# Twelve fewer products on TensorE: two blocks of the last recurrent head by Strassen's method, five steps of the recurrence shortened, token sums two blocks at once

## The chip, the cores and the metric

The kernel runs on one core of one Trainium2 chip. A core has five engines, each with its own instruction queue: TensorE (PE in the profile; its weight loads are shown apart as PEld), VectorE (DVE), ScalarE (ACT), GpSimd (POOL) and SyncE (SP), which issues nearly all DMAs. The engines run beside each other and wait for each other through semaphores; each queue is worked off strictly in the order in which it was written. The metric is device time in microseconds, from the first to the last instruction and the little that lies around it. Lower is better.

## The reference: what is computed

One layer of a hybrid encoder on 1024 tokens of width 1024, in float32. One wide projection of the tokens feeds two branches. Branch A is attention with 8 heads of 64 and a forget bias. Branch B is a gated linear recurrence with 4 heads of 128 channels:

```
f = lb + (1 - lb) * sigmoid(f_b)          # forget gate, per head and channel
q = silu(q_b);  k = 1 - f;  v = i_b
S_t = diag(f_t) S_(t-1) + k_t v_t^T;  o_t = S_t^T q_t
o = o * rsqrt(mean(o^2) + eps) * norm_g * sigmoid(g_b)
merged = sigmoid(gate_a) * (y_a @ w_pa) + sigmoid(gate_b) * (y_b @ w_pb)
x1 = layer_norm(ALPHA * x + merged @ w_o)
out = layer_norm(ALPHA * x1 + (silu(x1 @ w_g) * (x1 @ w_u)) @ w_ff_out)
```

The float32 products are made of three products of reduced-precision halves: each operand is split into a high part (`hi`, a cast on ACT) and a remainder (`lo`, a subtraction on DVE), and `mm3` adds hi·hi, hi·lo and lo·hi in PSUM.

## The kernel before

Tokens lie along the free dimension, 512 per PSUM bank, and channels on the 128 partitions. Most matrix products use one level of Strassen's method: seven products of half size in place of eight, with sums of operands made beforehand by DVE. Per block of 128 output channels and all 1024 tokens a direct projection takes 2 token halves x 8 channel chunks x 3 = 48 matmuls of 128x512; two blocks taken together by Strassen's method take 7 products x 4 chunks x 3 = 84 in place of 96.

The program in order of its source:

- values for both branches (`v_mul`), forget gates;
- `qk_all` (L799): four Strassen steps (`qk_strassen`, L733), one for each pair of attention heads. A step pairs a query block with a key block of `w_qk`. It loads the two weight blocks (tags `hl` or `kb`, as `QORDER` says), makes seven stationary operands `Tqk...` (each a cast on ACT and a subtraction on DVE), adds the partial results and writes split queries and keys to DRAM (`qk_d`), from where each attention head loads them again;
- attention by head: scores (`s`), minimum, exponential and row sums (`p`), transposes (`pt`), and the weighted values (`pv`);
- the recurrence by head: `hgrn_project` (L906) projects forget gate (block 1), query (block 0) and output gate (block 2) directly into banks `bps1`, `bps0`, `bps2`; `hgrn` (L934) forms cumulative log gates `b` by scans (eight of 128 tokens), then pair terms on seven levels (`level`, L975, each with four products `lp` that are put into `at` under a mask; the last level, neighbouring tokens, is `neighbours`, L1000), state terms (`up`, `box`) and outputs (`op`), which are normed (`ob`) and transposed (`ot`). Heads 0 to 3 follow each other, with `hgrn_project` of the next head between;
- parts of the merge gates (`gate_part`, `ge`), the rest of them by Strassen (`gs`);
- branch projections (`pps`), gating, and `merged` (L1256), which splits the token sums into operands for the output projection, one 128-channel block at a time; the output projection (`oa`, `ob`), layer norm and transposes (`x1t`), the feed-forward part (`fa` to `fe`, then `p`).

The source order is not the order on the engines. Every call is recorded by `Plan`, with the tiles it reads and writes. `schedule` places all calls by a table of costs (cost per operation, a delay of 400 ns before each TensorE call that depends on another engine, DMAs one after another); `improve` (L355) does this 36 times with ranks from the latest allowed start and random slack, and keeps the order that ends first by these costs. That order is then written out, engine by engine. So any change of the calls, or of the random seed, moves instructions nearly everywhere. Buffers are reused by tag: a new tile of a tag waits until an old one has been read for the last time.

Since each call is issued by one helper, nearly all instructions carry the same line, L387 (L388 after the change); tiles tell them apart. A float32 matmul that is not a transpose is shown as two records.

Of the kernel before, what the change touches and what calls it, by code (L numbers as in the profile page):

```python
# [9 lines left out]
BF16 = mybir.dt.bfloat16  # L10
U16 = mybir.dt.uint16
AF = mybir.ActivationFunctionType
# [51 lines left out]
class Plan:  # L64
# [326 lines left out]
def trunk(ctx: ExitStack, tc, a: dict, out: bass.AP):  # L391
# [340 lines left out]

    def qk_strassen(p, wtags, btags, last=False):  # L733
# [16 lines left out]

        def put(b, hf, o):
            hi, lo = (half("gt" if n else "tt", f"qk{p}_{b}{hf}{n}", F32R) for n in range(2))
            if b == 0:
                act.activation(hi, o, AF.Copy, scale=-0.125)
                dve.scalar_tensor_tensor(lo, o, -0.125, f(hi), op0=ALU.mult, op1=ALU.subtract)
            else:
                split(hi, lo, o)
            for n, t in enumerate((hi, lo)):
                sync.dma_start(qk_d[p, 2 * b + n, :, hs(hf)], f(t))

# [38 lines left out]
    def qk_all():  # L799
        for p, w, b in QORDER:  # L800
            qk_strassen(p, (w, w), b, p == QORDER[-1][0])

# [79 lines left out]

    once = keep([P, P + 1], "once", F32R)
    raw = half("gt", "once_r")
    sync.dma_start(raw[:, :P + 1], a["once"])
    act.copy(once, raw[:, :P + 1])
    reset, ones = f(once)[:, :P], once[:, 1:]
    lmask = const("lmask", [P, 2, MASKS], U16, "mask")
# [45 lines left out]
    def hgrn(h, qfg, box):  # L934
# [40 lines left out]
        def level(li):  # L975
# [17 lines left out]

            if li:
                m = lmask[:, :, 4 * nw - 7:8 * nw - 7, None].to_broadcast([P, 2, 4 * nw, L])
            else:
                m = lmask[:, :, :1, None].to_broadcast([P, 2, 4, L])
            dve.copy_predicated(across(at, L, 1), m, halves(lp, L))

        def neighbours():  # L1000

            low = take("hl", [2, NB], f"nb{h}", F32R)
            hi, lo = low[:, 0, :], low[:, 1, :]
            pr, e = (half("ph", f"nb{n}{h}") for n in "pe")
            b2 = b.rearrange("p (n a) -> p n a", a=2)
# [52 lines left out]
        for hf in range(2):  # L1058
# [197 lines left out]
    def merged(c, k, hf):  # L1256
        if not k and hf:
            return
        r11, r21 = (mraw[0][:, c, hs(i)] for i in range(2))
        r12, r22 = (mraw[1][:, c, hs(i)] for i in range(2))  # L1260
        op = (M11, M12, M22)[k + hf]
        split(op[0][:, c], op[1][:, c], (r11, r12, r22)[k + hf])
        if k and hf:
            s1 = half("tt", f"ms1r{c}")
            dve.tensor_add(s1, r21, r22)
            split(MS1[0][:, c], MS1[1][:, c], s1)
            dve.tensor_sub(r22, s1, r11)
            dve.tensor_sub(r12, r12, r22)
            dve.tensor_sub(r21, r11, r21)
# [100 lines left out]
    for i in (1,):  # L1370
# [6 lines left out]
        for fb in range(KC):  # L1377
# [5 lines left out]
            for hf in range(2):  # L1383
                sg = gated(i, fb, hf)
                o = bank(CYC[nbank % 5], f"pps{i}_{fb}_{hf}")
                nbank += 1
                project(o, w, hf, 4, lambda c: (yh[c], yl[c]))
                dve.tensor_mul(sg, o, sg)
                dve.tensor_add(mf[:, hs(hf)], mf[:, hs(hf)], sg)
                merged(fb % 4, fb // 4, hf)  # L1390
            if fb == 3:
# [88 lines left out]
    def from_raw(name, r):  # L1480
        op = operand("x", name)
        for c in range(4):
            split(op[0][:, c], op[1][:, c], r(c))
        return op
# [416 lines left out]
def _constants():  # L1901
# [3 lines left out]
    causal = np.tile(np.concatenate([causal, causal.T], axis=1), (1, NT // 2))  # L1905
    once = np.ones((P, P + 1), np.float32)
    once[:, 0] = 0
    lmask = np.zeros((P, 2, MASKS), np.uint16)
    for L in LEVELS:
# [86 lines left out]
```

## Time and profile before

| | |
|---|---|
| Median of 3 runs | 1412.66 us (1412.26 to 1413.19) |
| Profiled execution: its time, its span | 1412.1 us, 1410.3 us |
| Mean granted TensorE clock | 0.999 |
| PE, DVE, ACT, POOL busy share | 99%, 82%, 50%, 6% |
| First projection steps for attention (85 to 160 us) | PE 75.00, DVE 52.00, ACT 35.99 us busy |
| Attention (160 to 316 us) | PE 155.48, DVE 132.75, ACT 133.21 us busy |
| Recurrence (316 to 498 us) | PE 182.00, DVE 165.41, ACT 132.52 us busy |
| DMA | 245.23 MB, 174 GB/s on average |

The stages are cut where the trace shows the first score products, the last attention split and the end of the last recurrent head. Busy times of one engine are to be set against the length of the stage. The chain of work that ended last has 79% of the span on PE by the page's summary and DVE with 1%; the remaining pieces are short.

### The profile page before, as it was taken

Reading aid. Unit: us, or ns where it says so; the run is one execution under the profiler, and the core shown is the slowest. Engines: PE = TensorE matmul, PEld = TensorE weight load, DVE = VectorE, ACT = ScalarE, POOL = GpSimd, SP = SyncE. Lnnn points to the kernel's source line nnn. Section 1 sums busy time; section 2 is a strip of 40 time slices with the busy share of each in tenths; the row PEclk is TensorE's granted clock in tenths of the full one; section 3 lists DMA queues with packets and bytes.
Section 4 is the critical chain, followed back from the end, with each engine's and each line's share of the span. In section 5 each row is a group of like instructions: output and inputs, shape, how many; then the busy total and the mean of one; then the engine's idle time right before and its main releaser. Section 6 shows DMA issues by size and latency. Waiting matters only on the chain.

```text
span 1410.3 us, 19118 instructions
## 1 busy us (share of the span) xinstructions
PE 1399.7 (99%) x6650; PEld 1162.8 (82%) x6650; DVE 1161.6 (82%) x2025; ACT 710.5 (50%) x1275; POOL 87.3 (6%) x108
## 2 busy tenths in 40 slices
PE   9999999999999999999999999999999999999997
PEld 7788888888888888888887888888888888888886
DVE  7995878899998979778998879877687976699597
ACT  5534689887687632365439842233223334434330
POOL 0000133420000000000001000000000000000001
PEclk9999999999999999999999999999999999999999
DMA  7458999811113686456644637533334336878632
GB/s 274 156 167 271 301 291 259 243 61 45 46 53 113 215 254 196 134 165 220 231 131 140 208 103 227 181 117 100 98 106 141 112 112 209 315 249 284 216 122 90
DMA packets 99503, 245.23 MB, mean 174 GB/s; under 512 B 11456, under 2 KB 12736, under 8 KB 99408
## 3 DMA queue, kind: packets, MB, share of 16 engines
q1 hardware_dynamic: 98256, 239.83, 52.2%
q0 software_dynamic: 1152, 4.19, 1.6%
q8 instruction: 52, 0.85, 0.2%
q14 instruction: 43, 0.35, 0.1%
HBM read 181.26 MB, written 62.72 MB: 173 GB/s over the span
## 4 chain that ended last, share of the span: by engine, by line
PE 79%; DVE 1%; issue 0%; DVEq 0%
PE p L387 15%; PE fb L387 12%; PE gs L387 9%; PE fc L387 8%; PE bps L387 7%; PE fa L387 5%; PE fe L387 3%; PE pps L387 3%; PE oa L387 3%; PE ob L387 2%; PE ge L387 2%; PE lp L387 2%; PE op L387 1%; PE pv L387 1%; PE pt L387 1%; PE x1t L387 0%
## 5 line engine op out<-in xcount | busy, mean ns | idle before, releaser
L387 PE MATMUL p<-dp 128*128 128x512 f32 (+1 forms) x957 | 210.0, 382 | 0.0
L387 PEld LDWEIGHTS p<-dp 128*128 128x128 f32 x957 | 175.3, 188 | 34.8
L387 PE MATMUL fc<-xs,Tp 128*128 128x512 f32 x528 | 129.1, 389 | 0.0
L387 PE MATMUL fb<-xs,Tp 128*128 128x512 f32 x528 | 127.8, 389 | 0.0
L387 ACT CAST Tp<-t 128x512 fp32r<-128x512 f32 x88 | 54.4, 620 | 128.9 <-PE fb L387 69.1
L387 PEld LDWEIGHTS fc<-xs,Tp 128*128 128x128 f32 x528 | 99.0, 188 | 20.8 <-ACT Tp L387 0.3
L387 PEld LDWEIGHTS fb<-xs,Tp 128*128 128x128 f32 x528 | 99.1, 188 | 20.6
L387 DVE TENSOR_TENSOR Tp<-t,Tp 128x512 fp32r<-128x512 f32 x88 | 60.3, 689 | 30.9 <-ACT Tp L387 30.3
L387 PE MATMUL fa<-x,Tp 128*128 128x512 f32 x336 | 81.4, 389 | 0.0
L387 PE MATMUL bps<-xl,wb_h 128*128 128x512 f32 x192 | 77.1, 402 | 0.0
L387 PE MATMUL bps<-xh,wb_h 128*128 128x512 f32 x192 | 76.6, 401 | 0.0
L387 PE MATMUL bps<-xh,wb_l 128*128 128x512 f32 x192 | 76.2, 400 | 0.0
L387 PEld LDWEIGHTS fa<-x,Tp 128*128 128x128 f32 x336 | 63.1, 188 | 13.1
L387 ACT CAST dp<-dap 128x1024 fp32r<-128x1024 f32 (+1 forms) x42 | 41.2, 980 | 58.8 <-PE p L387 35.6
L387 POOL TENSOR_TENSOR norm<-norm,few 128x1 f32<-128x1 f32 x16 | 13.3, 830 | 902.8 <-DVE norm L387 882.9
L387 DVE TENSOR_TENSOR dp<-dap,dp 128x1024 fp32r<-128x1024 f32 (+1 forms) x42 | 47.5, 1132 | 22.4 <-ACT dp L387 22.4
L387 DVE TENSOR_TENSOR tl<-pt,th 128x512 fp32r<-128x512 f32 (+1 forms) x96 | 52.1, 551 | 8.9 <-PE pv L387 4.2
L387 PE MATMUL fb<-x,Tp 128*128 128x512 f32 x240 | 57.8, 389 | 0.0
L387 ACT CAST th<-pt 128x512 fp32r<-128x512 f32 (+1 forms) x96 | 45.4, 477 | 16.5 <-PE pt L387 9.8
L387 PEld LDWEIGHTS fb<-x,Tp 128*128 128x128 f32 x240 | 45.0, 188 | 9.4
L387 DVE TENSOR_TENSOR u<-fb,p 128x512 f32<-128x512 f32 x40 | 27.6, 690 | 22.7 <-PE fb L387 22.5
L387 PEld LDWEIGHTS bps<-xl,wb_h 128*128 128x128 f32 x192 | 36.2, 189 | 6.3
(1006 smaller groups left out, 3594.8 us busy)
## 6 DMA issues: line engine op xcount, KB each, us to landing
dbp<-in_w_fo SPq DMA_DIRECT2D x45, 512.0 KB, 4.8
dap<-a_d SPq DMA_DIRECT2D x35, 512.0 KB, 4.8
wg_r<-in_w_ff SPq DMA_DIRECT2D x22, 512.0 KB, 3.9
wu_r<-in_w_ff SPq DMA_DIRECT2D x22, 512.0 KB, 3.9
a_d<-ar SPq DMA_DIRECT2D x42, 256.0 KB, 3.0
wop_r<-in_w_o SPq DMA_DIRECT2D x18, 512.0 KB, 3.7
a_d<-as SPq DMA_DIRECT2D x33, 256.0 KB, 3.5
qk_d<-qk SPq DMA_DIRECT2D x32, 256.0 KB, 4.8
```

The lines of the kernel that those rows point to most:

```text
L387: getattr(q.engine, method)(*args, **kw)
```

## The change

**Five steps in place of four.** `QORDER` gets a fifth entry. An entry with two pairs names two blocks of the recurrence's weights, here block (1, 3), the forget gate of head 3, and (0, 3), its query. The step takes them through the same seven products. Its `put` applies the sigmoid (and for the query multiplies by the projection), and writes the result to a new DRAM tensor `hb_d`. `hgrn_project(3)` then loads both with one DMA each and projects only the output gate itself. The order of steps and their buffers change too: steps use `hl`, `kb`, `hl`, `kb`, `hl` in turn.

**Shorter steps of the recurrence.** (1) Four scans over 256 tokens replace eight over 128; `once` has zeros at columns 0 and 128 and so restarts the sum; the zeroing of four columns by POOL comes after the scans. (2) The first level copies its two halves on ACT in place of a masked copy on DVE. (3) Neighbouring tokens use the gate itself, as 1 - k, in place of a difference of `b` and an exponential. (4) The query is `Silu` in one ACT call, without a DVE product (heads 0 to 2). (5) The outputs are normed by four ACT calls of 128 columns per half with a scale per token, in place of one DVE product.

**Merged tokens.** `merged` and `from_raw` treat two blocks (1024 elements per partition) with one call each; `merged` runs after every second block.

**Small ones.** Masks are 8-bit in place of 16-bit. The matrix of ones that is the stationary operand of the diagonal and neighbour sums is read from one column with step zero. The planner's seed is 3 in place of 1.

The core of the diff:

```diff
-QORDER = ((0, "hl", ("s", "pt", "s")), (1, "kb", ("h", "pv", "h")), (2, "hl", ("s", "pt", "s")), (3, "hl", ("h", "s", "h")))
+QORDER = (((0,), "hl", ("s", "pt", "s")), ((1,), "kb", ("h", "pv", "h")), (((1,3), (0,3)), "hl", ("s", "pt", "s")), ((2,), "kb", ("h", "pv", "h")), ((3,), "hl", ("h", "pv", "h")))
+APART = {w: n for n, w in enumerate(w for x in QORDER if len(x[0]) == 2 for w in x[0])}
...
-        vary = np.random.default_rng(1)
+        vary = np.random.default_rng(3)
...
-            sync.dma_start(t, a["w_qk"][b, p])
+            sync.dma_start(t, a["w_qk"][b, pair[0]] if len(pair) == 1 else a["w_b"][pair[b]])
...
         def put(b, hf, o):
+            if len(pair) == 2:
+                t = half("gt", f"hp{p}_{b}{hf}")
...
+                act.activation(to, o, AF.Sigmoid)
+                if pair[b][0] == 0:
+                    dve.tensor_mul(to, o, to)
+                sync.dma_start(d, t)
+                return
...
-    reset, ones = f(once)[:, :P], once[:, 1:]
+    reset, ones = f(once), once[:, 1:2].to_broadcast([P, P])
...
         for bi, dst in ((1, fk), (0, q), (2, sg)):
+            if (bi, h) in APART:
+                sync.dma_start(dst, hb_d[APART[bi, h]])
+                continue
...
-                act.activation(d, o, AF.Sigmoid)
-                if bi == 0:
-                    dve.tensor_mul(d, o, d)
+                act.activation(d, o, AF.Sigmoid if bi else AF.Silu)
...
+        for n in range(4):
+            o, two = n // 2, slice(2 * n * P, 2 * (n + 1) * P)
+            dve.tensor_tensor_scan(b[:, two][:, o:], reset[:, :2 * P - o], fk[:, two][:, :2 * P - o], 0.0,
+                                   op0=ALU.mult, op1=ALU.add)
         pool.memset(bw[:, 1, :, 0:1], 0.0)
-        for w in range(NT):
-            o = w % 2
-            dve.tensor_tensor_scan(b[:, place(w)][:, o:], reset[:, :P - o], fk[:, place(w)][:, :P - o], 0.0,
-                                   op0=ALU.mult, op1=ALU.add)
...
+            if not li:
+                to, got = across(at, L, 1), halves(lp, L)
+                for c in range(2):
+                    act.copy(to[c * L:(c + 1) * L, c], got[c * L:(c + 1) * L, c])
+                return
...
-            dve.tensor_sub(e, b2[:, :, 1], b2[:, :, 0])
-            act.activation(e, e, AF.Exp)
...
-            dve.tensor_mul(pr, pr, e)
-            split(hi, lo, pr)
+            dve.scalar_tensor_tensor(by2(pr), across(k, 1, 1), 1.0, by2(pr), op0=ALU.subtract, op1=ALU.mult)
+            act.activation(hi, pr, AF.Copy, scale=-1.0)
+            dve.scalar_tensor_tensor(lo, pr, -1.0, f(hi), op0=ALU.mult, op1=ALU.subtract)
...
-            dve.tensor_mul(ob.rearrange("p (w t) -> p w t", t=P), op.rearrange("p (w t) -> p w t", t=P),
-                           rr[:, :, None].to_broadcast([P, 4, P]))
+            for w in range(4):
+                act.activation(ob[:, blk(w)], op[:, blk(w)], AF.Copy, scale=rr[:, w:w + 1])
...
-    lmask = np.zeros((P, 2, MASKS), np.uint16)
+    lmask = np.zeros((P, 2, MASKS), np.uint8)
```

What the planner made of it, at three places. First TensorE in the recurrence of head 2, where the products of level 1 (`lp2_1`) stand among the projections of head 3. The numbers behind `bps` are block, head and token half. Before:

```order
L387 MATMUL bps1_3_0_1126<-xl0_68,wb1_3_h0_1122 128x512
L387 MATMUL lp2_0_1084<-qe2_0_1083,ke2_0_1082 128x128 x4
L387 MATMUL bps1_3_0_1126<-xh0_66,wb1_3_l0_1123 128x512
L387 MATMUL lp2_1_1087<-qe2_1_1086,ke2_1_1085 128x128 x4
L387 MATMUL bps1_3_0_1126<-xh0_66,wb1_3_h0_1122 128x512
L387 MATMUL bps1_3_0_1126<-xl0_68,wb1_3_h0_1122 128x512
```

With the change:

```order
L388 MATMUL bps2_3_0_1151<-xh0_66,wb2_3_h0_1147 128x512
L388 MATMUL lp2_1_1113<-qe2_1_1112,ke2_1_1111 128x128 x4
L388 MATMUL bps2_3_0_1151<-xl0_68,wb2_3_h0_1147 128x512
L388 MATMUL bps2_3_0_1151<-xh0_66,wb2_3_l0_1148 128x512
L388 MATMUL bps2_3_0_1151<-xh1_67,wb2_3_h1_1149 128x512
L388 MATMUL bps2_3_0_1151<-xl1_69,wb2_3_h1_1149 128x512
```

The forget gate and query of head 3 are gone from here; the output gate of head 3 stands in their place, and parts of the merge gates (`ge`) follow where that is used up.

Second the DMA queue of SP at the end of the second step (`qk1`): the names are `qk` step, operand and half; `hp2` are the results of the step with two recurrent blocks, `q2`, `k2`, `kl` the loads of attention head 0. Before:

```order
L387 DMA qk_d_189<-qk1_110_248 128x512
L387 DMA q2_0_324<-qk_d_189 64x1024 x2
L387 DMA v_d_180<-v4_185 128x1024
L387 DMA k2_0_325<-qk_d_189 64x1024 x2
L387 DMA kl_0_326<-qk_d_189 64x1024
L387 DMA qk_d_189<-qk1_111_249 128x512
L387 DMA kl_0_326<-qk_d_189 64x1024
```

With the change:

```order
L388 DMA q2_0_352<-qk_d_189 64x1024
L388 DMA hb_d_190<-hp2_11_279 256x1x256
L388 DMA qk_d_189<-qk1_110_249 128x512
L388 DMA q2_0_352<-qk_d_189 64x1024
L388 DMA qk_d_189<-qk1_011_258 128x512
L388 DMA v_d_180<-v5_186 128x1024
L388 DMA hb_d_190<-hp2_01_285 256x1x256
L388 DMA k2_0_353<-qk_d_189 64x1024 x2
```

The stores of the new step stand among the loads of head 0.

Third ACT in the recurrence of head 2, around its query (`hbq2`). `ACT_TABLE_LOAD` changes the function table. Before:

```order
L387 ACT_TABLE_LOAD
L387 ACTIVATE hbq2_1047<-bps0_2_0_1062 128x2x2x128
L387 CAST wb2_2_h0_1065<-wb2_2_r_1064 128x512
L386 ACT_TABLE_LOAD
L387 ACTIVATE kd2_1077<-hbb2_1072,tot_1073 128x128
L387 ACTIVATE box1_106<-box1_106 128x8x64 x2
```

With the change:

```order
L388 ACTIVATE ob1_1_1070<-op1_1_1068,ss_1069 128x128 x4
L388 ACTIVATE box1_106<-box1_106 128x32x16
L388 ACTIVATE box1_106<-box1_106 128x64x8 x2
L388 ACTIVATE dec_1100<-tot_1099 128x8
L388 ACT_TABLE_LOAD
L388 ACTIVATE hbq2_1073<-bps0_2_0_1088 128x2x2x128
L388 ACTIVATE hbq2_1073<-bps0_2_1_1089 128x2x2x128
```

Both halves of the query now follow one table load, and the scaling of the outputs (`ob1_1<-op1_1,ss`) stands on this engine. In the whole program there are 38 table loads before and 30 with the change.

More of the change, by code (lines that the diff above doesn't have):

```diff
@@ L10 @@
 BF16 = mybir.dt.bfloat16
-U16 = mybir.dt.uint16
+U16 = mybir.dt.uint8
 AF = mybir.ActivationFunctionType
@@ L758, in put @@
             for n, t in enumerate((hi, lo)):
-                sync.dma_start(qk_d[p, 2 * b + n, :, hs(hf)], f(t))
+                sync.dma_start(qk_d[pair[0], 2 * b + n, :, hs(hf)], f(t))
         mul("p1", b11, oa, True)
@@ L799, in qk_all @@
     def qk_all():
-        for p, w, b in QORDER:
-            qk_strassen(p, (w, w), b, p == QORDER[-1][0])
+        for p, (pair, w, b) in enumerate(QORDER):
+            qk_strassen(p, pair, (w, w), b, p == len(QORDER) - 1)
     scored = []
@@ L880, in attention @@
                 sync.dma_start(ya_d[p, i].rearrange("a d t -> (a d) t")[:, hs(g)], y)
-    once = keep([P, P + 1], "once", F32R)
+    once = keep([P, 2 * P], "once", F32R)
     raw = half("gt", "once_r")
-    sync.dma_start(raw[:, :P + 1], a["once"])
-    act.copy(once, raw[:, :P + 1])
-    reset, ones = f(once)[:, :P], once[:, 1:]
+    sync.dma_start(raw[:, :2 * P], a["once"])
+    act.copy(once, raw[:, :2 * P])
+    reset, ones = f(once), once[:, 1:2].to_broadcast([P, P])
     lmask = const("lmask", [P, 2, MASKS], U16, "mask")
@@ L1003, in neighbours @@
             hi, lo = low[:, 0, :], low[:, 1, :]
-            pr, e = (half("ph", f"nb{n}{h}") for n in "pe")
-            b2 = b.rearrange("p (n a) -> p n a", a=2)
-            dve.tensor_sub(e, b2[:, :, 1], b2[:, :, 0])
-            act.activation(e, e, AF.Exp)
+            pr = half("ph", f"nbp{h}")
             def by2(t):
@@ L1258, in merged @@
             return
-        r11, r21 = (mraw[0][:, c, hs(i)] for i in range(2))
-        r12, r22 = (mraw[1][:, c, hs(i)] for i in range(2))
+        two = slice(c, c + 2)
+        r11, r21 = (mraw[0][:, two, hs(i)] for i in range(2))
+        r12, r22 = (mraw[1][:, two, hs(i)] for i in range(2))
         op = (M11, M12, M22)[k + hf]
-        split(op[0][:, c], op[1][:, c], (r11, r12, r22)[k + hf])
+        split(op[0][:, two], op[1][:, two], (r11, r12, r22)[k + hf])
         if k and hf:
[L1264 to L1267, printed above, removed]
+            dve.tensor_add(r22, r21, r22)
+            split(MS1[0][:, two], MS1[1][:, two], r22)
+            dve.tensor_sub(r22, r22, r11)
             dve.tensor_sub(r12, r12, r22)
@@ L1481, in from_raw @@
         op = operand("x", name)
-        for c in range(4):
-            split(op[0][:, c], op[1][:, c], r(c))
+        for c in range(0, 4, 2):
+            split(op[0][:, c:c + 2], op[1][:, c:c + 2], r(slice(c, c + 2)))
         return op
@@ L1905, in _constants @@
     causal = np.tile(np.concatenate([causal, causal.T], axis=1), (1, NT // 2))
-    once = np.ones((P, P + 1), np.float32)
-    once[:, 0] = 0
-    lmask = np.zeros((P, 2, MASKS), np.uint16)
+    once = np.ones((P, 2 * P), np.float32)
+    once[:, ::P] = 0
+    lmask = np.zeros((P, 2, MASKS), np.uint8)
     for L in LEVELS:
```

19 lines of the change are left out of this document (13 added, 6 removed).

## The prediction

> **What bounds the kernel now.** I read the summary of the page first, then who TensorE waited for, then busy time by stage.
>
> ```profile
> span 1410.3 us, 19118 instructions
> PE 1399.7 (99%) x6650; PEld 1162.8 (82%) x6650; DVE 1161.6 (82%) x2025; ACT 710.5 (50%) x1275; POOL 87.3 (6%) x108
> ```
>
> PE is busy for all but 10.6 us. Since a busy PE need not be a PE at its peak, the waits of PE come next:
>
> ```profile
> engine line waited for: us in total, times, longest us
> PE vy L387 <- DVE few L387: 1.2, 1, 1.2
> PE vx L387 <- ACT xh L387: 0.8, 1, 0.8
> PE oa L387 <- ACT Top4h L387: 0.6, 1, 0.6
> PE s L387 <- DVE soft L387: 0.3, 1, 0.3
> PE pt L387 <- DVE tl L387: 0.3, 1, 0.3
> ```
>
> PE waits 3.2 us in all. 2.0 of them are at the start, which the change leaves alone; 1.2 us lie in what is planned anew. So the list of matmuls is the time, and a matmul taken out is time taken out, as long as no wait comes in. The stages show its price and how near the other engines are:
>
> ```profile
> core 0: us, PE busy (x) PEld busy (x) DVE busy (x) ACT busy (x) POOL busy (x), PEclk, DMA share, GB/s
> 85.00:160.00 75.00, 75.00 (x335) 61.95 (x334) 52.00 (x95) 35.99 (x69) 1.98 (x2) 1.00 0.78 247
> 160.00:316.00 156.00, 155.48 (x902) 132.83 (x901) 132.75 (x418) 133.21 (x288) 56.49 (x72) 1.00 0.78 226
> 316.00:498.00 182.00, 182.00 (x1017) 157.11 (x1016) 165.41 (x269) 132.52 (x266) 15.40 (x14) 1.00 0.30 100
> 735.00:805.00 70.00, 69.31 (x334) 55.00 (x333) 59.41 (x110) 64.11 (x126) 5.11 (x8) 1.00 0.49 162
> 840.00:1080.00 240.00, 240.00 (x1061) 198.72 (x1060) 192.92 (x302) 72.69 (x122) 0.00 (x0) 1.00 0.42 134
> ```
>
> From 840 to 1080 us there is nothing but 128x512 matmuls at full clock. 1061 records are touched, two of them cut by the edges, so 1060 intervals: 240.00 / 1060 = 0.2264 us for one. In attention (second row) DVE and ACT have 85% each, in the recurrence (third) DVE has 91%: no engine is over its stage's length, but the margins are what the change has to live in.
>
> What the notes say of this price stands apart: the Trainium skill, "TensorE: Matmul & The Clock Gate", section "Back-to-back issue gap", gives about 131 ns per matmul of 512 columns in a stream of load and multiply pairs. The trace does not agree (226.4 ns over 1060 of them); by the page the twelve matmuls below would be worth 1.6 us and the time would be 1411.1, no change that can be told, and with the row against it I give that no chance of its own.
>
> **The change part by part.**
>
> *Strassen for two blocks.* 96 matmuls of 128x512 become 84, the only change of the number of matmuls: 12 x 0.2264 = 2.72 us less on PE. This lies wholly on the path.
>
> What moves with it: in the built order PE has 335 matmuls from the first query step to the first score in place of 228; 30 fewer long ones between the first score and the last weighted value (108 to 85 of the steps, 187 to 185 projections, 29 to 24 `ge`, one diagonal sum), 6.8 us; and 86 fewer after that to the last recurrent transpose (projections 389 to 295, `ge` 115 to 120, `gs` 44 to 47), 19.5 us. So attention shrinks to 156.0 - 6.8 = 149.2 us of PE, the recurrence to 182.0 - 19.5 = 162.5. Whether DVE and ACT shrink as well decides the rest:
>
> ```profile
> L387 DVE TENSOR_TENSOR wb_l<-wb_r,wb_h 128x512 fp32r<-128x512 f32 x24 | 18.1, 759 | 2.3 <-ACT wb_h L387 2.0 <-PE bps L387 0.3
> L387 DVE COPY_PREDICATED at<-lmask,lp 128x512 f32<-128x512 uint16 x24 | 19.8, 823 | 2.9 <-PE lp L387 2.7
> L387 DVE TENSOR_TENSOR hbq<-bps,hbq 128x512 f32<-128x512 f32 x8 | 5.5, 691 | 4.9 <-ACT hbq L387 4.8
> L387 DVE TENSOR_TENSOR ob<-op,ss 128x512 f32<-128x512 f32 x8 | 5.5, 684 | 0.9 <-POOL ss L387 0.9
> L387 DVE TENSOR_TENSOR nbe<-hbb 128x512 f32<-128x512 f32 x4 | 2.8, 690 | 0.0
> L387 DVE TENSOR_TENSOR_SCAN hbb<-once,hbf 128x128 f32<-128x128 f32 x16 | 7.2, 450 | 0.0
> L387 DVE TENSOR_TENSOR_SCAN hbb<-once,hbf 128x127 f32<-128x127 f32 x16 | 6.9, 434 | 0.0
> L387 DVE TENSOR_TENSOR Tqk0p1l<-wq_r,Tqk0p1h 128x512 fp32r<-128x512 f32 x1 | 0.7, 683 | 0.0
> ```
>
> DVE loses in the recurrence, over four heads: weight splits of two blocks 8 x 0.759 = 6.1; query products 8 x 0.691 = 5.5; output scaling 8 x 0.684 = 5.5; one of six masked level copies per head 4 x 0.823 = 3.3; neighbour differences 4 x 0.690 = 2.8. The scan over 256 is not in the trace: between 0.450 (a second half for nothing) and 0.884 (two old ones), 16 of them against 14.1 us; I take the middle, 3.4 us less. Sum 26.6 us (23.2 to 30.3). Of that some 24 lie after attention: (165.4 - 24) / 162.5 = 87%, against 91% before. The new step gives DVE about 16 instructions (seven splits, four weight sums, three additions, two products) at 0.69, 11 us, in a stage where DVE has 52.00 of 75.00 and which gets 24 us longer.
>
> ```profile
> L387 ACT ACT_TABLE_LOAD x17 | 21.8, 1283 | 0.3
> L386 ACT ACT_TABLE_LOAD x17 | 21.8, 1283 | 0.3
> L387 ACT CAST wb_h<-wb_r 128x512 fp32r<-128x512 f32 x24 | 14.8, 617 | 7.6 <-PE bps L387 5.7 <-ACT hbq L387 0.9 <-PE qk_h L387 0.9
> L387 ACT ACTIVATE ob<-op 128x128 f32<-128x128 f32 x32 | 8.4, 276 | 8.6 <-PE op L387 8.6
> L387 ACT ACTIVATE nbe<-nbe 128x512 f32<-128x512 f32 x4 | 2.5, 631 | 0.0
> L387 ACT CAST th<-pt 128x256 fp32r<-128x256 f32 x16 | 5.9, 366 | 1.8 <-PE pt L387 1.4 <-DVE soft L387 0.4
> L387 ACT ACTIVATE hbg<-bps 128x512 f32<-128x512 f32 x8 | 4.6, 602 | 0.0
> ```
>
> ACT loses 8 table loads (38 to 30 in the order) x 1.283 = 10.3, weight casts 8 x 0.617 = 4.9, exponentials 4 x 0.631 = 2.5. It gains the scaling, 32 calls at about 0.276 (the squares of the same PSUM columns), 8.8, and two level copies of 64x256 per head, 8 x 0.366 (a cast of 256 PSUM columns) = 2.9. Net 6.0 less. The four sigmoids (0.602) move to the new step with seven casts and three copies, 8.5 us in the stage with 36 of 75. I cost all of this at nothing: PE's own list is the cover, in each stage at least as much as before.
>
> The zeroing by POOL now stands behind the scans and before the first use of `b`, a new handover to POOL and back. Its price is the 0.1 us memset and two semaphores; the nearest row is the wait for POOL ahead of `ob`, 0.9 us over eight. For four heads 0 to 0.5 us on DVE, under PE: nothing. The 8-bit masks: between nothing and the gap from a masked copy (0.823) to a plain product (0.690), 24 x 0.133 = 3.2 us either way, on DVE: nothing.
>
> *Ones with step zero.* 24 weight loads read one column 128 times:
>
> ```profile
> L387 PEld LDWEIGHTS dg<-qkh,once x8: 186/187/188, 307.6 to 454.7; 128*128 128x128 f32 x8
> L387 PEld LDWEIGHTS lp_nb<-nb,once x8: 187/188/189, 341.0 to 472.7; 128*128 128x128 f32 x8
> ```
>
> At 0.188 they hide under the matmul ahead (0.226). Twice as long they would show 0.15 each, 3.6 us in all; no row speaks for that, so 0, with 3.6 as an end.
>
> *DMAs.* Four stores of 256 KB and two loads of 512 KB are new, 2.1 MB; the weights of the two blocks, 1 MB, are loaded with the query steps and no longer in the recurrence.
>
> ```profile
> GB/s 274 156 167 271 301 291 259 243 61 45 46 53 113 215 254 196 134 165 220 231 131 140 208 103 227 181 117 100 98 106 141 112 112 209 315 249 284 216 122 90
> ```
>
> From 106 to 282 us (slices 4 to 8) the queue runs at up to 301 GB/s; 3.1 MB more cost 10 us there, and the first score moves 24 us later on PE. Nothing on the path; the ends are 0 and the rival below.
>
> *Merged tokens.* 28 splits of 512 become 14 of 1024, and 16 sums become 8.
>
> ```profile
> L387 DVE TENSOR_TENSOR ms<-m,ms 128x512 fp32r<-128x512 f32 x12 | 7.8, 684 | 0.0
> L387 DVE TENSOR_TENSOR wos<-wop_r,wos 128x1024 f32<-128x1024 f32 x4 | 4.9, 1218 | 0.0
> L387 ACT CAST ms<-m 128x512 fp32r<-128x512 f32 x12 | 6.9, 619 | 13.0 <-PE oa L387 6.8 <-DVE m L387 5.6 <-PE ob L387 0.6
> L387 ACT CAST Top3h<-wop_r 128x1024 fp32r<-128x1024 f32 x2 | 2.1, 1056 | 4.5 <-PE oa L387 3.7 <-PE ob L387 0.8
> ```
>
> DVE saves 22 x (2 x 0.684 - 1.218) = 3.3 us, ACT 14 x (2 x 0.619 - 1.056) = 2.5 us. A pair is ready about 1 us later than its first block was; the first product, 48 matmuls or 10.9 us, stands ahead of the next operand and covers it. Two pairs of the last operand (`ms3`) come just ahead of the layer norm, where ACT has 64.11 of 70 us and PE waited 0.6 for `Top4h`: 0.36 us less ACT there; I let 0.4 of that wait go.
>
> *Sum.* 1412.1 - 2.7 - 0.4 = 1409.0 against the profiled execution, which lies 0.6 under the median of the runs; on the median 1412.66 - 3.1 = 1409.5.
>
> **The rivals.** (A) The mixed stages give more: the remaining 0.8 us of replanned waits go, and up to 2 us of small losses that the modelled ends of matmuls hide between short and long ones: 1406.7 to 1408.5, say 1407.5. For it: DVE and ACT are lighter. Against: only 1.2 us of such waits are visible at all.
>
> (B) The gain is eaten by new waits of 1.5 to 5 us, so that the change does not do what it says: about 1412.5. Places: loads of attention heads behind the stores of the new step; the output chain of a head, where squares, POOL and now four scalings follow each other; weight loads with step zero. For it: a new order with new forms. Against: PE ran 182.00 of 182 us beside a DVE at 91%.
>
> (C) Slower: attention keeps its length. It loses 6.8 us of PE's long matmuls, but nearly none of its softmax work: 133.21 us of ACT in 149.2 would be 89%. If exponentials and splits on ACT set the pace, PE idles 6.8 us there: 1412.66 - 2.72 + 6.8 = 1416.7. It decides from about 90% of ACT in a stage where PE needs each result soon. For it: the stage from 735 to 805 us, with ACT at 92%, is the one with the `Top4h` wait. Against: DVE at 91% cost PE nothing in the recurrence.
>
> **How the numbers follow.** 0.2% is 2.8 us and about what a measurement of this kernel can tell from no change; the line to "faster" is at 1409.83, just above the forecast. Forecast (PE's list less twelve, waits within 1.4 us of this): 0.55, of it 0.38 under the line and 0.17 above. A: 0.12, faster. B: 0.20, no change. C: 0.13, slower. So faster 0.50, same 0.37, slower 0.13. The range 1407.0 to 1413.5 takes the forecast, nearly all of A and the nearer three quarters of B: 0.8.
>
> **What would show it.** The trace after should have twelve fewer long matmuls and PE still at 99%; PE waits of 2.5 to 3.5 us; weight loads of `once` still at 0.188; DVE near 1143 us (1161.6 - 26.6 + 11 - 3.3) and ACT near 708 (710.5 - 6.0 - 2.4 + 8.5 - 2.5); 30 table loads; attention about 149 and recurrence about 162 us long. The prediction is wrong if PE waits for `th`, `p` or `s` by microseconds between 185 and 340 us (C), if `hbf`, `hbq` or head loads release PE (B), or if the 128x512 interval is not 0.226.

## The result, and the profile after

The changed kernel takes 1422.07 us (median of 4 runs, 1420.42 to 1422.64) against 1412.46 us beside it on the same chip: a ratio of 1.0065, 95% interval 1.0053 to 1.0077. It is 9.6 us slower, where 1409.5 was forecast, a range up to 1413.5, and a chance of 0.13 for slower. The profiled execution took 1422.64 us, 10.5 more than the profiled one of before (1412.1). One repeat each of two kernels tried below (2365 and 2363 us, mean granted clock 0.556) and one of the kernel before (1753 us, 0.752) are left out of the medians.

The head of the page after, and the list of what TensorE waited for:

```profile
span 1420.9 us, 19112 instructions
PE 1402.9 (99%) x6638; PEld 1164.1 (82%) x6638; DVE 1153.3 (81%) x1975; ACT 709.4 (50%) x1295; POOL 91.1 (6%) x108
```

```profile
PE pv L388 <- ACT th L388: 3.1, 1, 3.1
PE pv L388 <- ACT ya L388: 2.6, 2, 1.9
PE gs L388 <- ACT ys1h L388: 1.5, 1, 1.5
PE vy L388 <- DVE few L388: 1.2, 1, 1.2
PE oa L388 <- ACT Top4h L388: 1.0, 1, 1.0
PE x1t L388 <- ACT r L388: 0.7, 1, 0.7
PE pt L388 <- DVE tl L388: 0.4, 1, 0.4
```

The twelve matmuls are gone (6638 against 6650), but PE waits 10.5 us in place of 3.2. Busy time by stretch shows where; first the changed kernel, then the same work in the kernel before (columns as in the prediction: PE, PEld, DVE, ACT, POOL, granted clock, DMA share, GB/s):

```profile
200.00:220.00 20.00, 17.69 (x104) 14.94 (x103) 14.45 (x54) 14.96 (x33) 7.30 (x12) 1.00 1.04 277
220.00:240.00 20.00, 16.23 (x80) 13.37 (x80) 10.97 (x34) 12.71 (x23) 6.30 (x7) 0.91 0.99 289
185.00:334.00 149.00, 142.92 (x822) 122.03 (x822) 119.47 (x382) 120.83 (x268) 57.53 (x69) 0.99 0.78 214
340.00:502.00 162.00, 162.00 (x931) 140.54 (x929) 143.93 (x225) 124.54 (x280) 16.73 (x14) 1.00 0.33 108
515.00:535.00 20.00, 18.54 (x82) 15.08 (x81) 16.36 (x25) 5.59 (x10) 0.00 (x0) 1.00 0.88 238
740.00:790.00 50.00, 48.28 (x224) 37.73 (x224) 39.37 (x73) 39.56 (x75) 4.71 (x7) 0.97 0.35 116
860.00:1080.00 220.00, 220.00 (x973) 182.20 (x972) 175.52 (x276) 66.59 (x111) 0.00 (x0) 1.00 0.43 139
```

```profile
200.00:220.00 20.00, 20.00 (x120) 17.25 (x120) 16.92 (x59) 18.06 (x38) 7.62 (x10) 1.00 0.93 260
220.00:240.00 20.00, 20.00 (x120) 17.25 (x119) 17.11 (x60) 19.06 (x46) 7.18 (x9) 1.00 0.96 272
733.00:783.00 50.00, 49.31 (x240) 38.86 (x238) 40.25 (x77) 42.98 (x83) 4.49 (x7) 1.00 0.39 125
```

Three places make up nearly all of it. Idle time is the stretch less PE's busy time, and a granted clock of 0.91 over 20 us is 0.09 x 20 = 1.8 us of lost clock:

| stretch of the changed kernel | idle, us | lost clock, us | before, us | extra, us |
|---|---|---|---|---|
| 200 to 240, second head of attention | 6.1 | 1.8 | 0.0 | 7.9 |
| 515 to 535, behind the recurrence | 1.5 | 0.0 | 0.0 (no PE wait there) | 1.5 |
| 740 to 790, layer norm and output product | 1.7 | 1.5 | 0.7 | 2.5 |

In the second place the chain of work that ended last runs through a load of attention's result, issued late (behind a weight load that could go only at 517.8 us) and 6.7 us under way:

```profile
518.78 6.69 DMA ys<-ya_d
```

Together 11.9 of the 13.2 us that have to be found (10.5 slower, and 2.7 of matmuls gone); the other 1.3 us are not placed.

The first place, step by step. What stopped ScalarE, what stopped PE behind it (timeline; in brackets the idle time and its releaser), and how long the stores took from issue to landing (`ya_d` between 185 and 240 us, `qk_d` between 215 and 220 us):

```profile
211.49 0.58 ACT L388 COPY ya<-pv 128x512 f32<-128x512 f32 x1 [3.02 <-DMA ya_d<-ya]
226.07 0.58 ACT L388 CAST th<-pt 128x512 fp32r<-128x512 f32 x1 [3.76 <-DMA qk_d<-qk]
```

```profile
212.13 0.51 PE L388 MATMUL pv<-th,vhl 128*128 128x512 f32 x1 [1.94 <-ACT ya L388]
226.70 0.50 PE L388 MATMUL pv<-th,vhl 128*128 128x512 f32 x1 [3.09 <-ACT th L388]
```

```profile
L388 SPq DMA_DIRECT2D ya_d<-ya x4: 320/323/530, 197.3 to 238.7; - x4
DMA to landing us min/median/max: 7.7/8.1/14.1
...
L388 SPq DMA_DIRECT2D qk_d<-qk x2: 319/320/320, 217.4 to 218.1; - x2
DMA to landing us min/median/max: 8.5/8.5/8.5
```

A copy of `ya` needs one of two `gt` buffers, a cast of `th` one of four `tt` buffers, and the stores of the query and key steps hold buffers of the same two tags until they land. With the queue full (share 1.04 and 0.99) a store of 256 KB takes 8 to 14 us here, ScalarE stands still for 3.0 and 3.8 us on a buffer (from 208.47 and 222.31 us on), and PE, which has 1.7 and 1.3 us of other work left then, stops behind it at 210.19 and 223.61. In the kernel before, in the same window, the stores of `ya` landed in 3.7 us (median) and nobody waited for one:

```profile
DMA to landing us min/median/max: 2.0/3.7/8.5
```

The stop costs more than its length, for the clock falls after it:

```profile
224.00:226.00 2.00, 0.00 (x0) 0.00 (x0) 0.00 (x0) 0.00 (x0) 0.00 (x0) 1.00 1.08 268
226.00:228.00 2.00, 1.30 (x6) 1.07 (x7) 1.32 (x4) 1.93 (x5) 0.00 (x0) 0.97 1.05 302
228.00:230.00 2.00, 2.00 (x8) 1.66 (x7) 1.87 (x7) 2.00 (x6) 0.03 (x1) 0.50 1.05 256
230.00:232.00 2.00, 2.00 (x9) 1.71 (x8) 0.86 (x2) 1.81 (x4) 2.00 (x3) 0.67 1.03 244
```

The third place has the same shape with smaller idle times: between 763 and 766 us PE is busy for 1.35 of 3 us (waits for `Top4h`, 1.0, and for `r`, 0.7), and from 767.5 to 770 us it runs at half clock.

```profile
763.00:766.00 3.00, 1.35 (x6) 0.71 (x5) 3.00 (x5) 2.71 (x6) 0.00 (x0) 1.00 0.00 1
767.50:770.00 2.50, 2.50 (x8) 1.94 (x7) 2.50 (x5) 2.47 (x6) 0.00 (x0) 0.50 0.00 0
```

### The profile page after: what moved, and what is told of

The parts are those of the page before. It is cut to its first block, busy times and chain, and to the rows that moved or that the text cites. A ratio compares the mean times of both kernels' runs of the same rounds, so it can differ in the third digit from the quotient of the medians.

```text
span 1420.9 us, 19112 instructions
## 1 busy us (share of the span) xinstructions
PE 1402.9 (99%) x6638; PEld 1164.1 (82%) x6638; DVE 1153.3 (81%) x1975; ACT 709.4 (50%) x1295; POOL 91.1 (6%) x108
## 4 chain that ended last, share of the span: by engine, by line
PE 95%; DMA 3%; DVE 2%; ACT 0%; issue 0%; SPq 0%; DVEq 0%; ACTq 0%
PE p L388 15%; PE fb L388 12%; PE fc L388 8%; PE gs L388 8%; PE bps L388 8%; PE fa L388 5%; PE vx L388 4%; PE qk_h L388 3%; PE fe L388 3%; PE oa L388 3%; PE pps L388 3%; PE vy L388 3%; PE qk_s L388 2%; PE ge L388 2%; PE pv L388 2%; PE pt L388 2%
## 5 line engine op out<-in xcount | busy, mean ns | idle before, releaser
L388 PE MATMUL bps<-xh,wb_h 128*128 128x512 f32 x160 | 65.3, 408 | 0.0
L388 PE MATMUL bps<-xh,wb_l 128*128 128x512 f32 x160 | 64.3, 402 | 0.0
L388 DVE TENSOR_TENSOR tl<-pt,th 128x512 fp32r<-128x512 f32 (+1 forms) x96 | 51.5, 552 | 15.6 <-ACT th L388 11.9
L388 PE MATMUL bps<-xl,wb_h 128*128 128x512 f32 x160 | 64.0, 400 | 0.0
L388 POOL TENSOR_SCALAR p<-p,sums 128x128 f32<-128x128 f32 (+7 forms) x48 | 35.8, 758 | 127.5 <-DVE sums L388 97.0
```

What stands on the lines that cost most here:

```text
L388: getattr(q.engine, method)(*args, **kw)
```

## The experiments

Theories at the start. *Stores*: the fifth query step pushes the last stores into the loads of the heads. *Order*: the planner drew a poor order, and the same contents in another order are as fast as before. *Forms*: one of the new forms of instruction costs the time. Each number below is a median, with the ratio to the kernel before on the same chip.

**Parts alone, and other draws of the planner's random numbers.**

The step alone in the kernel before (the diff of the first part of the change, nothing else):

> The kernel before with the Strassen step for the two blocks of the last head alone; every other edit is left out. If the stores of the fifth step cost the time (they push the query and key stores into the head loads, ScalarE waits for buffers, TensorE idles behind it), this has the loss without the other edits: 1412.5 - 2.7 + 8 to 13 = 1418 to 1423 us, with ScalarE waiting for DMA by microseconds between 195 and 235 us. If the loss is a matter of the newly planned order, anything from 1408 to 1422 with the idle time elsewhere. If the new forms cost it (ones with step zero, 8-bit masks, copies on ScalarE, merged splits), 1409.7 us, the list of matmuls less twelve.

Without the step, all else changed:

```diff
-QORDER = (((0,), "hl", ("s", "pt", "s")), ((1,), "kb", ("h", "pv", "h")), (((1,3), (0,3)), "hl", ("s", "pt", "s")), ((2,), "kb", ("h", "pv", "h")), ((3,), "hl", ("h", "pv", "h")))
+QORDER = (((0,), "hl", ("s", "pt", "s")), ((1,), "kb", ("h", "pv", "h")), ((2,), "hl", ("s", "pt", "s")), ((3,), "hl", ("h", "s", "h")))
```

> The changed kernel with the query and key steps as before (four of them), so that the last head's gates and queries are projected block by block; all else is kept, the planner's seed too. Stores of the fifth step to blame: 1411 to 1413 us, no wait of ScalarE for a store over 1 us before 235 us. Planned order to blame: anything, 1408 to 1422. New forms to blame: 1422 + 2.7 = 1424.8 us.

The changed kernel with the seed of before, and the kernel before with the seed of the changed one:

```diff
-        vary = np.random.default_rng(3)
+        vary = np.random.default_rng(1)
```

> The changed kernel with the planner's random numbers from the seed of before (1 in place of 3). Stores to blame: 1418 us or more, and ScalarE still waits 2 us or more for a store between 195 and 235 us. Order to blame: the time moves by 5 us or more, to 1409 to 1417 or above 1427, and the waits stand elsewhere or are gone. New forms to blame: 1422 within 1.5 us.

> The kernel before with the planner's random numbers from the seed of the changed kernel (3 in place of 1). Stores to blame or new forms to blame: 1412.5 within 2 us, since neither is in it. Order to blame: it can move by 5 us or more as well, to 1418 and above.

Measured: the step alone 1422.33 us (ratio 1.0066, 1.0052 to 1.0080); without it 1418.08 (1.0043, 1.0029 to 1.0056); the changed kernel with seed 1 1415.85 (1.0022, 1.0014 to 1.0031); the kernel before with seed 3 1416.00 (1.0023, 1.0014 to 1.0032). *Forms* alone falls: the same forms in another order take 6.2 us less. *Order* is real: the kernel before loses 3.3 us to a mere draw. What the step itself does could not be told from these kernels, which change contents and draw together. So the next runs keep the order.

The step alone was run once more for its trace (1423.57 us):

> The kernel before with the step for two blocks alone, once more, for its trace. If the step's collision of stores and head loads made its 1422.5 us, ScalarE waits for stores (qk_d or ya_d) by 2 us or more between 195 and 235 us, and nothing is lost near 520 us or between 740 and 790 us beyond what before lost there (1.5 and 0.4). If the order makes the loss, it lies somewhere else.

ScalarE waited 1.4 us for `qk_d` and PE 2.0 us for `tl` in attention, less than expected, with a clock of 0.96 over 200 to 240 us; the larger loss was in the recurrence, where DVE has 148.87 of 160 us (93%) and PE waits for the weights that DVE and ScalarE split:

```profile
340.00:500.00 160.00, 155.71 (x886) 133.84 (x885) 148.87 (x245) 112.30 (x235) 14.46 (x13) 0.99 0.31 99
```

```profile
PE ge L388 <- ACT we_h L388: 2.5, 1, 2.5
PE ge L388 <- DVE we_l L388: 0.7, 1, 0.7
```

A reading that fits, though these are single draws: the step takes matmuls out of the recurrence that covered DVE there, and the other edits, which make DVE lighter, make up for it. With them PE is busy all of 162.00 us there, with DVE at 143.93 (89%).

**The order kept, one cause taken away.**

Two weight loads of 512 KB, first used at 220 and 250 us in the planner's order, are issued behind the first store of `ya` and no longer ahead of it; no other instruction moves (`find` gives SP's call with such an output and source):

```diff
+MOVED = ((("we10_r", ""), ("qk_d", "qk4_101")), (("wb0_0_r", ""), ("qk_d", "qk4_101")))
         order = self.improve(slack, wait)
+        turn = [i for _, i in order]
...
+        for late, behind in MOVED:
+            i, m = find(*late), find(*behind)
+            turn.remove(i)
+            turn.insert(turn.index(m) + 1, i)
```

> The changed kernel with its order as it is on every engine but SP, where two weight loads of 512 KB (the gate block split at 250 us in the plan, and the head-0 block split at 220 us) are issued behind the stores of the last step at 199 us and no longer at 195 and 196 us, ahead of the first store of ya. If the queue's backlog ahead of that store is what stops ScalarE (3.0 us) and then TensorE, the store lands 3.5 us earlier (1.05 MB at 289 GB/s, 14.1 to about 10.6 us), the wait of ScalarE for ya_d goes to under 0.5 us, the later one for qk_d shrinks too, and the time falls by 4 to 8 us to 1414 to 1418. If TensorE's idle time there comes from ScalarE's own load (softmax, the fifth step's copies), the time stays at 1422 within 1.5 us.

1420.29 us (1.0054, 1.0039 to 1.0069): 1.8 less than the changed kernel's, where 4 to 8 was expected. Since the two intervals overlap, 1.8 can't be told from nothing, and in the trace the stretch from 200 to 240 us loses more than before the move (5.9 us idle at a clock of 0.91, against 6.1 at 0.96). The store landed early enough and the first wait was gone, but the next copy of `ya` hit the next store:

```profile
208.49 0.60 ACT L401 COPY ya<-pv 128x512 f32<-128x512 f32 x1
...
221.96 0.59 ACT L401 COPY ya<-pv 128x512 f32<-128x512 f32 x1 [4.51 <-DMA ya_d<-ya]
...
226.07 0.59 ACT L401 CAST th<-pt 128x512 fp32r<-128x512 f32 x1 [2.94 <-DMA qk_d<-qk]
```

ScalarE ran 3.0 us ahead from 208.49 on, only to stop 4.5 us at 221.96 for the store issued at 213. A wait taken away here comes back at the next buffer, since the queue is full from 200 to 240 us and every store in it is late.

Then the bytes of the step itself:

```diff
             for _, i in order:
+                if q.name == "SP" and args[1].tensor.name.startswith("hp2_1"):
+                    continue
+                if q.name == "SP" and args[0].tensor.name.startswith("hbq3"):
+                    args = args[0], self.instead
```

> The changed kernel, order kept on all engines, without two of the four new stores (the queries of the last head; they are left out of the computation, and its query tile is filled with a weight block instead). If the bytes of the new stores fill the queue, 0.5 MB less gives 1.8 us or more back and the first ya store lands earlier. If it is only what is issued after 185 us that counts, nothing changes: 1422 within 1.5 us, and the ya store still takes 13 us or more.

1420.81 us (1.0056, 1.0043 to 1.0069), with ScalarE waiting 3.7 us each for `ya_d` and `qk_d`, much as in the changed kernel, and the first `ya` store at 14.1 us as before. The time is 1.3 us lower, again within the intervals. So nothing shows that the new stores, issued between 141 and 159 us, are in the way. And the last step's query stores, on top of the two loads issued later:

```diff
+                if q.name == "SP" and args[1].tensor.name.startswith("qk4_0"):
+                    continue
+                if q.name == "SP" and args[0].tensor.name[:5] in ("q2_6_", "q2_7_"):
+                    args = args[0], self.instead[args[1].offset]
```

> The kernel with the two loads issued later (1420.3 us), order kept, and without the four stores of the last step's queries (heads 6 and 7 read the queries of heads 4 and 5 instead: that part of the computation is wrong in it). If ScalarE stops because the buffers of th and ya are held by stores that the full queue lands late, two of these stores are the ones th waited for: that wait (2.9 us) goes, the wait for ya_d (4.5 us) shrinks or goes, and 5 to 8 us are gained: 1412 to 1415. If TensorE would idle there anyway, for ScalarE's own load, under 2 us are gained: 1418.5 to 1420.5.

1418.99 us (1.0047, 1.0033 to 1.0060). The wait for `qk_d` is gone, as it should be, but the one for `ya_d` stands as it was:

```profile
ACT ya L405 <- DMA ya_d<-ya: 4.5, 1, 4.5
```

So the buffer mechanism holds, wait by wait; what was wrong was that taking away two of its occasions would be enough. By both steps the time fell by 3.1 us, with intervals that still overlap, and the stretch from 200 to 240 us loses 3.8 us of idle time at a clock of 0.96, 5.4 us in place of 7.9.

**The step in another place.**

```diff
-QORDER = (((0,), "hl", ("s", "pt", "s")), ((1,), "kb", ("h", "pv", "h")), (((1,3), (0,3)), "hl", ("s", "pt", "s")), ((2,), "kb", ("h", "pv", "h")), ((3,), "hl", ("h", "pv", "h")))
+QORDER = (((0,), "hl", ("s", "pt", "s")), ((1,), "kb", ("h", "pv", "h")), ((2,), "hl", ("s", "pt", "s")), ((3,), "kb", ("h", "pv", "h")), (((1,3), (0,3)), "hl", ("h", "pv", "h")))
```

> The changed kernel with the step for the two blocks of the last head put fifth in place of third, so that the stores of query and key steps end one step earlier and what the last step stores (1 MB in place of 2 MB) is wanted by nobody before the recurrence. If the late query and key stores and their buffers are the cause, the loss between 200 and 240 us goes: 1422 - 8 = 1414 (1411 to 1417), ScalarE no longer waits for qk_d there. If the place of the step doesn't matter and any fifth step costs this, 1420 to 1424.

1415.38 us (1.0018, 1.0009 to 1.0027): 6.7 us less than with the step third, same seed. In the trace, of a repeat that took 1413.05 us, ScalarE waits for no DMA in that stretch, and `ya` lands in 5.6 us (median); what is left there is PE's own wait for a key load:

```profile
220.00:240.00 20.00, 20.00 (x126) 17.30 (x125) 16.17 (x62) 17.96 (x43) 7.67 (x10) 1.00 0.88 254
```

```profile
PE s L388 <- DMA kl<-qk_d: 1.5, 1, 1.5
```

The planner draws a new order for this kernel too, so this run alone doesn't say whether the place or the draw did it; the seeds below bear on that.

**The merged tokens**, alone in the kernel before, and undone in the kernel with the step last:

```diff
-        split(op[0][:, c], op[1][:, c], (r11, r12, r22)[k + hf])
+        split(op[0][:, two], op[1][:, two], (r11, r12, r22)[k + hf])
```

> The kernel before with the splits and sums of the merged tokens over two blocks alone. If these forms make the two waits ahead of the layer norm (Top4h, r) and the half clock after them, 2 to 3 us more are lost between 740 and 790 us: 1414.5 to 1416. If that loss is chance of the order, 1412.7 within 1 us or anything with idle time elsewhere; if the saving of the forms counted, 1412.3.

> The kernel with the two-block step put last (1415.5 us), and merged tokens split and summed block by block as before. If the two-block forms make the loss between 740 and 790 us (3.9 there in that kernel against 2.3 before), 1.5 to 2 us are gained: 1413.5 to 1414. If that loss comes with the newly planned order and not with the forms, the time stays within 1 us of 1415.5 or moves by what another order gives, to 1410 at best.

Alone 1413.68 us (1.0007, 0.9998 to 1.0016), no difference that can be told; undone beside the step in last place 1411.62 (0.9995, 0.9986 to 1.0004), 3.8 less than with it. There PE is busy for all but 0.7 us between 740 and 790, at full clock, and for all of 200 to 240 us:

```profile
200.00:240.00 40.00, 40.00 (x244) 34.88 (x243) 33.60 (x114) 36.43 (x79) 16.79 (x22) 1.00 1.03 282
740.00:790.00 50.00, 49.34 (x239) 38.33 (x239) 41.53 (x78) 45.32 (x91) 5.72 (x6) 1.00 0.48 162
```

(PE's idle time in this stretch was 1.7 us in the kernel with the step last and 0.7 in the kernel before, not the 3.9 and 2.3 that the expectation names.) That the wide forms cost the third place its 2.5 us is not shown: alone they left 0.7 us of idle time there. Beside the other edits, PE idles 1.2 to 1.8 us there in all six draws with the wide forms, and 0.7 to 1.3 in the nine draws with single blocks, four of them of the kernel before; the clock fell there in two of the fifteen, both with the wide forms.

**How much is the draw.** Two more seeds for each kernel, and three for the one with the step last and the merged tokens block by block:

> The changed kernel with a third seed for the planner (2). Contents to blame (stores and loads of five steps, two-block forms): 1415 to 1423 us, with 4 us or more lost between 190 and 240 us or 740 and 790 us beyond what before lost there. Order to blame: anywhere from 1409.5 to 1422, below 1413 as likely as above.

> The changed kernel with a fourth seed for the planner (4). Contents to blame: 1415 to 1423 us; order to blame: 1409.5 to 1422, below 1413 as likely as above.

> The kernel before with a third seed (2). Contents to blame: 1412 to 1416 us, all draws of before under all draws of the changed kernel. Order to blame: 1411 to 1420, overlapping with the draws of the changed kernel.

> The kernel before with a fourth seed (4). Contents to blame: 1412 to 1416 us, under all draws of the changed kernel. Order to blame: 1411 to 1420, overlapping with them.

> As the run with the step last and the merged tokens block by block, with the planner's seed of before. List of matmuls less twelve with the small losses of before gives 1409.5 to 1410; chance of the order gives anything from there to 1417.

> Step last, merged tokens block by block, third seed (2). If the place of the step and the narrow forms take away what the contents cost, the twelve matmuls show: 1415.4 (mean of the four draws of before) - 2.7 = 1412.7, so 1410 to 1415.5. If they don't matter, as the draws of the changed kernel: 1414.5 to 1422.

> Step last, merged tokens block by block, fourth seed (4): 1410 to 1415.5 us if the place of the step and the narrow forms matter, 1414.5 to 1422 if they don't.

| seed | before, us | changed, us | step last, single blocks, us |
|---|---|---|---|
| 1 | 1412.66 | 1415.85 | 1414.77 |
| 2 | 1415.14 | 1416.25 | 1413.74 |
| 3 | 1416.00 | 1422.07 | 1411.62 |
| 4 | 1418.01 | 1414.82 | 1412.87 |
| mean | 1415.5 | 1417.2 | 1413.3 |

The groups overlap. The kernel before stands on the best of its four draws and the changed kernel on the worst of its four. By the means the contents cost 1.8 us, with a standard error of 1.9 over the four pairs (3.2, 1.1, 6.1, -3.2): not to be told from nothing, and not the gain of 2.7 either. (A pair shares its seed and no more: other contents give another order.) With the step last and single blocks the kernel is faster than the changed one in all four pairs (by 1.1 to 10.5 us; 4.0 in the mean, standard error 2.2), and 2.2 us below the mean of before, standard error 1.6: about the twelve matmuls, though four draws don't prove it. No draw beat the kernel before as it stands by more than can be measured; the best, 1411.62, has a ratio of 0.9995 with 1 inside its interval.

The draws also say what the loss from 200 to 240 us hangs on. All four draws of the changed kernel have the step third. Where seed 3 lost 7.9 us, seeds 1, 2 and 4 (in this order) lose 1.0 to 1.1, at full clock and with the queue as full:

```profile
200.00:240.00 40.00, 38.88 (x233) 33.59 (x233) 31.94 (x110) 35.42 (x73) 14.82 (x19) 1.00 1.02 303
200.00:240.00 40.00, 38.86 (x228) 32.95 (x228) 30.01 (x103) 34.91 (x75) 15.47 (x20) 1.00 0.99 294
200.00:240.00 40.00, 38.96 (x237) 33.54 (x236) 32.47 (x116) 33.68 (x74) 15.69 (x22) 1.00 1.01 295
```

With seed 1 the last query and key stores are issued even later than with seed 3 (223.8 us against 218.1), and the stores of `ya` take as long (median 8.1 us), yet the only wait for a store there is one of 0.6 us by DVE. So neither the place of the step nor late stores by themselves make the loss. What the trace of seed 3 has beside them is that the next copy and cast of ScalarE want just the buffers that such stores hold.

## Why the prediction was wrong

*Where it held.* Twelve matmuls fewer, at 220.00 / 972 = 0.2263 us each between 860 and 1080 us: -2.7 us of PE's list. DVE and ACT have less work in the recurrence: DVE 143.93 us, 89% of 162.00 (87% was expected), ACT 124.54 us; PE is without a wait. The small forms came out within 0.1 us of their terms, and none is seen on the path:

```profile
L388 ACT ACT_TABLE_LOAD x17 | 21.8, 1283 | 1.0 <-PEq L2007 0.7
L387 ACT ACT_TABLE_LOAD x13 | 16.7, 1283 | 0.2
L388 DVE COPY_PREDICATED at<-lmask,lp 128x512 f32<-128x512 uint8 x20 | 16.7, 836 | 0.7 <-PE lp L388 0.6
L388 DVE TENSOR_TENSOR_SCAN hbb<-once,hbf 128x255 f32<-128x255 f32 (+1 forms) x16 | 11.8, 761 | 2.3 <-ACT hbf L388 2.2
L388 ACT ACTIVATE ob<-op,ss 128x128 f32<-128x128 f32 x32 | 9.1, 374 | 0.0
L388 PEld LDWEIGHTS dg<-qkh,once 128*128 128x128 f32 x8 | 1.5, 188 | 0.3
```

30 table loads as counted; the 8-bit mask at 0.836 against 0.823; the scan over two blocks at 0.761 against a middle of 0.667; the scaling on ACT at 0.374 where 0.276 was taken; weight loads with step zero at 0.188. ACT's total was forecast at 708 and is 709.4; DVE's at 1143 and is 1153.3, 10 us off, but under PE.

*The step that failed first* is the one on the DMAs: "Nothing on the path". It counted bytes (3.1 MB, 10 us of queue) and compared them with a stage. What counts is when a store lands whose buffer is wanted: in this order, with the head loads bunched ahead of it in a full queue, a store needs 8 to 14 us, and of the buffers there are two (`gt`) and four (`tt`). The bytes of the new stores are not shown to matter (half of them left out changed nothing that can be told). The last query and key stores moved from 181 to 218 us, into the loads of later heads, and of ScalarE's two long waits one is for such a store and one for a store of `ya`. Since seed 1 has these stores later still without the loss, they are not enough by themselves; it takes the order of this draw, and what in it decides was not isolated. The trace of before had shown the same queue at a share of 0.93 to 1.04 between 160 and 240 us with 0.3 us of idle time on PE; the prediction read that as room. 7.9 us of the loss are here.

*The second* is "PE's own list is the cover, in each stage at least as much as before". Over a stage that is right (162 us of PE over 144 of DVE). Over three microseconds it isn't: in attention PE waits for a copy of 0.6 us by ScalarE, and ScalarE for a buffer. A total says nothing of how far an engine runs ahead.

*The third* is the term of -0.4 us for the wait of `Top4h`. It went from 0.6 to 1.0, with 0.7 for `r` beside it and a fall of the clock: +2.5 us.

*What was missing* is the price of a wait. All rivals counted its length alone. Between 226 and 232 us the clock was at 0.97, 0.50 and 0.67, which makes 3.4 us at half clock and 1.7 us lost behind an idle time of 3.1. The Trainium skill, "TensorE: Matmul & The Clock Gate", section "Part 1: The HAM clock gate", has the array fall to half rate after an idle window of about 3.4 us and return after as long a busy one. The rate and the length of the slow time agree with these rows. The length of the stop does not: 3.1 us were enough here, and at 763 us, where PE was busy for 1.35 of 3 us, the clock fell all the same.

*The rivals.* B named the place ("loads of attention heads behind the stores of the new step") in the reverse order: stores stood behind the loads. Its price, 1.5 to 5 us, was too small, since the waits added up (from 3.2 to 10.5 us) and the clock came on top. C had the sign and the sign to look for (PE waiting for `th` and `ya` after 185 us), by a mechanism that the rows exclude: ScalarE has 120.83 of 149 us there (81%), under the 90% from which it was to decide, and stood still at the time. From the first score to the last weighted value attention took 177.6 us (165.4 to 343.0) against 176.8 before (141.2 to 318.0): the 6.8 us by which it was to shrink went into these waits and the slow clock.

*And the draw.* Any edit of this kernel has its order drawn anew, and four draws of one and the same contents lie 5.4 us apart for the kernel before and 7.3 for the changed one, about twice the gain that was forecast. The prediction took the order of before as the typical one, with "new waits" of at most 5 us; a kernel that stands on its best draw can mostly lose by a new one. Most of the 9.6 us is this, the best draw of one kernel set beside the worst of the other, and so bad luck for the forecast. The other three draws of the changed kernel lie 2.2 to 3.6 us above the kernel before as it stands, and level with the mean of its four draws.

## What to carry to other kernels

Cost a store by when its buffer is wanted again and what stands ahead of it in the queue, not by its bytes: at a queue share near 1.0 stores of 256 KB landed after 3.3 to 14.1 us in the draws above, and whether that costs anything is decided by who wants the buffer next. Taking one such wait away can hand it to the next buffer. A step whose results nobody wants soon may do better behind the ones that are wanted than between them: the run with it last points that way, but doesn't show it apart from the draw. Where a planner with random numbers sets the order, compare several draws of both versions before a difference of half a per cent is put down to the edit.

## What the runs showed of the hardware

A stop of PE of 3.1 us, and idle times of 1.65 us in 3 us with work between, were each followed by about 3.4 us at a granted clock of 0.50, 1.7 us lost. How long a single stop has to be is not one number: after 1.93 us of idle time before 212 us the clock fell in the run without half of the new stores (first row), and after 1.94 us at the same place in the changed kernel it did not (second row).

```profile
212.00:216.00 4.00, 4.00 (x13) 3.24 (x14) 1.16 (x4) 3.97 (x9) 0.84 (x1) 0.57 1.04 240
212.00:216.00 4.00, 3.58 (x18) 2.95 (x18) 1.94 (x8) 3.97 (x10) 0.69 (x1) 1.00 1.04 223
```

Stores of 256 KB on the same queue landed 2.0 us after issue at best (before) and 14.1 at worst (after). Repeats of one kernel in this family also spread more than those of before, 1412.9 to 1418.3 us with the step last against 1411.0 to 1415.2. In part this goes with the clock: with the step last, the three repeats under 1413.5 us have a mean granted clock of 0.999, and the two above 1417 us 0.996 and 0.997, an estimated 3 to 4 us of lost clock. What makes the clock fall in one repeat and not in another was not tried.
